# Four S5 output gates of layer 0 projected in the first stage, and the compressed queries cut into two jobs

## Chip, cores and metric

One Trainium2 chip, of which the kernel uses one core. The metric is the device time of one launch in microseconds (us), lower is better. Engines: PE (TensorE, matrix products and transposes), DVE (VectorE), ACT (ScalarE), POOL (GpSimd) and SP (SyncE), whose instruction stream issues nearly all DMAs. Every engine works through its own list in order; an instruction that waits holds up all that stand behind it on its engine.

## What is computed

A backbone of two layers over 512 latent tokens and 256 context tokens, width 1024, in float32. A layer feeds one modulated input to three branches: (A) a bidirectional S5 state-space layer with a GLU, (B) neighbourhood attention over an 8 x 64 grid with a learned bias, (C) latent attention (MLA) with compressed queries and keys. Each branch is projected to the model width, multiplied by a gate that is itself a projection of the input, and added:

```python
y = jax.nn.gelu(y)                                  # S5 output
y = y * jax.nn.sigmoid(y @ w_glu + b_glu)
...
IN_SPLITS = (SSM_WIDTH, SSM_WIDTH, NA_WIDTH, NA_WIDTH, NA_WIDTH, NA_WIDTH,
             MLA_Q_RANK, MLA_KV_RANK, MLA_ROPE_DIM, MLA_WIDTH, D_MODEL, D_MODEL, D_MODEL)
```

The last three slices of this projection are the gates of the branches. Then come an output projection, a residual and a layer norm. A second projection of the conditioning vector (`w_mod`) gives shift, scale and gate of each layer.

## The kernel before

**Numbers.** Each float32 operand is split into a high part (`hh`, `wh`, `ah`) and a low part (`hl`, `wl`, `al`), and a product is three matmuls (L232 for the projections, L1051 for the compressed ones). The high part is an ACT copy (L142), the low part a subtraction (L145) on DVE or POOL, as a table `SE` says for each stage; in the first stage of layer 0 every low part is DVE's. `wraw` (L215) loads 128 columns of weights into one of four `wr` buffers. A projection onto 128 channels is 8 x 3 matmuls of 512 columns and as many of 256.

**Stages of a layer.** First stage (`s5a`): projections of S5 inputs, gates and compressed queries, and, for layer 0, the S5 weight matrices, which DVE builds out of tables (tiles `sb`, with small PE products L659 and transposes L197 between them). Then neighbourhood attention and the S5 blocks (`na`), MLA (`mla`), the merge (`mrg`) and the output stage (`out`, L1608). In layer 0 the first stage takes about the first 239 us, the merge some 280 us up to 990 us.

**First stage.** `JOBS` (L108) is a string of letters for each layer, worked through from left to right: `u` S5 inputs, `a` and `m` gates of channels that are stored to DRAM (`za`, `zm`), `B` one S5 build, `N` the tables of the attention bias, `c` half of the compressed queries. `compressed(half)` first projects (L1051) and copies to `ct`, then computes an RMS scale on DVE, transposes `ct` in four groups on PE and stores the results (`rms_c` to `c`, `kpe` to `kr`).

**Merge of layer 0.** Branch b, then branch c, in eight steps each. Of the eight S5 gates (`ga`, columns `C_GA`) two are projected in the MLA stage and six after the merge's branch c (L1514 to L1517, each stored to `ga_d`). `SIDE` (L85) is one letter per step: `B` a build for layer 1, `N` the bias tables of layer 1 (loads L361, stores L363 to `na_zd`), `G` the function `gelu` of the S5 output. `gelu` closes the pool that builds and bias tables use, and takes its tiles from that memory. For each of four blocks it loads `y` (L1470, two buffers), squares (ACT), scales (DVE, L154), multiplies (POOL, L145), takes tanh (ACT), makes `gf` in nine pieces (DVE, L148), and splits it into `ah` (ACT) and `al` (DVE). The GLU follows: four groups of 24 matmuls over those four blocks, each with tanh, a product with `za` and a split. Then branch a: eight groups of 24 matmuls, gated by `ga`. `mod_step()` puts one piece of layer 1's `w_mod` product on PE (L306, four matmuls per 512 KB load L304) after each gate or group.

**Order.** The kernel is written in the order of these jobs; a scheduler of the framework then orders each engine's list by its own estimate of when things are ready, so that neighbouring jobs are interleaved. The list is fixed before the launch.

Of the kernel before, what the change touches and what calls it, by code (L numbers as in the profile page):

```python
# [15 lines left out]
AF = mybir.ActivationFunctionType  # L16
# [9 lines left out]
TOK = LAT + CTX  # L26
# [3 lines left out]
C_GA, C_GN, C_GM = 4000, 5024, 6048  # L30
# [51 lines left out]
SE = {'out0': (2, (1,)), 'out1': (2, (1,)), 'mla0': (4, (0,)), 'mla1': (2, (1,)), 's5a1': (1, (0,)), 'mrg0': (1, (0,))}  # L82
SE_REST = (3, (0,))

SIDE = ('T....B.B..N...G.........', '................G.......')  # L85

GX = ((0, 0, 1, 1), (1, 1, 1, 0))

# [16 lines left out]
TO = ((1024,), (1024,), (512, 512), (512, 512))  # L105
CE = 'VVA'

JOBS = ('uuBaBmaBmBacmaNmc', 'maaBmmaBcamucuuu')  # L108


G_NA = "na_q0 na_kh0 na_kl0 s5_u s5_s0 s5_s1 s5_w s5_rc s5_o s5_mg s5_va s5_vb s5_vp na_vc na_v na_z na_a na_b na_p na_pt na_q1 na_kh1 na_kl1"
# [8 lines left out]
def build(tc, a, out):  # L120
    nc = tc.nc
    V, S, P, PE = nc.vector, nc.scalar, nc.gpsimd, nc.tensor
    Q, PQ = nc.sync, nc.gpsimd
# [7 lines left out]
    def T(p, shape, tag, bufs=1, dt=F32):  # L131
        if isinstance(p, dict):
            p = p.get(tag, p[None])
        return p.tile(list(shape), dt, name=tag, tag=tag, bufs=bufs)
# [6 lines left out]
    def act(o, i, f=AF.Copy, **kw):  # L141
        return S.activation(out=o, in_=i, func=f, **kw)  # L142
# [14 lines left out]
    dr = pool("dr", DRAM)  # L157
# [669 lines left out]
    with st:  # L827
# [10 lines left out]
        for l in range(DEPTH):  # L838
            need_ctx = l < DEPTH - 1
            n_tok = TOK if need_ctx else LAT  # L840
# [16 lines left out]
            def project(c, with_ctx):  # L857
                wh, wl = wsplit(wraw(wi[:, c:c + 128], 8))
                return gemm(wh, wl, h_parts(with_ctx))
# [14 lines left out]
            def mod_step():  # L874
                next(later, None)

            u_d = []
            where[0] = f"s5a{l}"
            with phase("s5a", 3, 2, 1, 1) as sa:
                reserve(sa, [128, TOK], "z", 2)  # L880
# [25 lines left out]
                if l == 0:  # L906
                    sc = mod_prep(sa)
                    with tc.tile_pool(name="pre", bufs=1, reuse_waits="tile") as pre:
# [72 lines left out]
                        for q in range(4):  # L981
                            PQ.dma_start(out=dcols[32 * q:32 * q + 16].rearrange("i l b x -> i (l b) x"),
                                        in_=a["ssm_d"].rearrange("l (y x q i) -> q i (l y) x", x=2, q=4, i=16)[q])
# [49 lines left out]
                def compressed(half):  # L1033
# [7 lines left out]
                    for kc in range(4):  # L1041
# [3 lines left out]
                        for kk in range(2):  # L1045
                            k = 2 * kc + kk
# [30 lines left out]
                    for b in range(2):  # L1077
                        P.tensor_copy(  # L1078
                            out=ct[:, :, NC + 16 * b:NC + 16 * b + 16].rearrange("p j (s e) -> p j s e", s=2),
                            in_=ct[:, :, 384 + 16 * b:400 + 16 * b].rearrange("p j (s e) -> p j s e", s=2)[:, :, ::-1])  # L1080
                    for i in (3, 2, 0, 1):
                        n = 128 * (sum(with_q) if i < 2 else 3)
                        m = 64 if i == 3 else 128
                        q = pss()
                        for j in range(n // 128):
                            transpose(q[0:m, 128 * j:128 * j + 128], ct[:, j, 128 * i:128 * i + m])
                        tok = slice(384 * half, 384 * half + n)
                        if i < 3:
                            r = T(sp, [128, 384], "rms_c", 2)[:, 0:n]
                            act(r, q[:, 0:n], scale=gq[:, i:i + 1])  # L1090
                            Q.dma_start(out=c_d[i][:, tok], in_=r)
                            continue
                        nl = min(LAT - 384 * half, 384)
                        pe_t = T(sp, [32, 384], "kpe_t")
                        s = slice(384 * half, 384 * half + nl)
                        kpe = T(sp, [32, 384], "kpe")
                        tt(V, kpe[:, 0:nl], q[0:32, 0:nl], rope[0:32, s], ALU.mult)
                        tt(V, pe_t[:, 0:nl], q[32:64, 0:nl], rope[32:64, s], ALU.mult)
                        tt(V, kpe[:, 0:nl], kpe[:, 0:nl], pe_t[:, 0:nl], ALU.add)
                        if nl < 384:  # L1100
                            act(kpe[:, nl:384], q[0:32, nl:384])
                        Q.dma_start(out=kr_d[:, tok], in_=kpe)

                jobs = {"u": input_s5, "a": gate_a, "m": gate_m, "c": compressed, "B": build_s5, "N": biases}
                done = dict.fromkeys(jobs, 0)
                if l == 0:
                    done["u"] = NU
# [9 lines left out]
            with phase("na", 2, 2, 2, groups=G_NA) as nap:  # L1117
                for t in ("q", "kh", "kl"):
                    reserve(nap, [128, 2, TOK], f"na_{t}0", 1, FR)
                for i in range(4):  # L1120
# [30 lines left out]
                    z = T(nap, [128, TOK], "na_z", 2)  # L1151
# [110 lines left out]

            where[0] = f"mla{l}"
            with phase("mla", 2, 2, 2, groups=G_MLA) as mp:
                ga = {}
                exps = {}

                def gate_s(m):
# [23 lines left out]
                f = early((128, TOK), c_d[2])  # L1292
# [17 lines left out]
                for k in range(2):  # L1310
                    f = early((128, n_tok), c_d[k][:, 0:n_tok])
# [3 lines left out]
                for t in range(6):  # L1315
                    o = psg()
# [4 lines left out]
                for i in range(4):  # L1321
                    z = T(mp, [128, TOK], "mla_z", 2)
# [15 lines left out]
                    for k in range(2):  # L1338
                        Q.dma_start(out=uqv[:, k, :, 0:96],
                                    in_=a["mla_w_uq"][l, 128 * k:128 * k + 128, 192 * i:192 * i + 192]  # L1340
                                    .rearrange("p (h n) -> p h n", h=2))
                    for b in range(2):
                        V.tensor_copy(
                            out=uq[:, :, 96 + 16 * b:112 + 16 * b].rearrange("p k (s e) -> p k s e", s=2),
                            in_=uq[:, :, 64 + 16 * b:80 + 16 * b].rearrange("p k (s e) -> p k s e", s=2)[:, :, ::-1])
# [74 lines left out]
            with phase("mrg", 4, 3, 0, 1, groups=G_MRG) as mg, contextlib.ExitStack() as es:  # L1420
# [100 lines left out]
                for m2 in range(2):  # L1521
                    wh, wl = wsplit(wraw(a["ssm_w_glu"][l, :, 256 * m2:256 * m2 + 256], 4))
                    for r in range(2):
                        m = 2 * m2 + r
# [7 lines left out]
                        z = T(gp, [128, TOK], "za", 2)[:, 0:n_tok]  # L1532
# [21 lines left out]
            with phase("outp", 4, 4, 0, groups=G_OUT) as op:  # L1554
# [11 lines left out]
                for v in range(2 if need_ctx else 1):  # L1566
                    t = T(op, [128, D], f"gate{v}")
                    Q.dma_start(out=t.rearrange("p (k n) -> p k n", k=8),
                                in_=bass.AP(tensor=gd.tensor, offset=gd.offset + v * 128, ap=[[0, 128], [256, 8], [1, 128]]))
# [20 lines left out]
                for tl in range(6 if need_ctx else 4):  # L1590
# [12 lines left out]
                    for n in cols:  # L1603
                        c = slice(c0, c0 + n)
                        o = psg()[:, 0:n]
# [11 lines left out]
                    if last and LE[tl] == "A":  # L1617
                        normalise_act(op, r, r, (mean, rstd))
                        for n in range(2):
                            c = slice(512 * n, 512 * n + 512)  # L1620
# [46 lines left out]
```

## Time and profile before

| | us |
|---|---|
| runs shown, median (lowest, highest) | 1797.0 (1796.72, 1801.12) |
| the profiled execution, its own time | 1799.89 |
| span of the profiled execution | 1798.1 |
| PE busy | 1661.2 (92%) |
| DVE busy | 1239.1 (69%) |
| ACT busy | 747.0 (42%) |
| POOL busy | 482.3 (27%) |

The profiled execution took 2.9 us more than the median of the runs. The span begins with the first instruction profiled; all times of places below count from there. The mean granted clock of PE was 0.972 of full speed; by slices it lies at 1.00 or near 0.50, which are its two levels, 2.4 and 1.2 GHz. A matmul's row holds the time until its result is out, so rows of PE overlap: a step from start to start is what one costs.

### The profile page before, as it was taken

Reading aid. Unit: us, or ns where it says so; the run is one execution under the profiler, and the core shown is the slowest. Engines: PE = TensorE matmul, PEld = TensorE weight load, DVE = VectorE, ACT = ScalarE, POOL = GpSimd, SP = SyncE. Lnnn points to the kernel's source line nnn. Section 1 sums busy time; section 2 is a strip of 40 time slices with the busy share of each in tenths; the row PEclk is TensorE's granted clock in tenths of the full one; section 3 lists DMA queues with packets and bytes.
Section 4 is the critical chain, followed back from the end, with each engine's and each line's share of the span. In section 5 each row is a group of like instructions: output and inputs, shape, how many; then the busy total and the mean of one; then the engine's idle time right before and its main releaser. Section 6 shows DMA issues by size and latency. Waiting matters only on the chain. (4 is left out here: it accounts for less than half of the span.)

```text
span 1798.1 us, 29033 instructions
## 1 busy us (share of the span) xinstructions
PE 1661.2 (92%) x10808; PEld 1390.0 (77%) x10808; DVE 1239.1 (69%) x2653; ACT 747.0 (42%) x1466; POOL 482.3 (27%) x353
## 2 busy tenths in 40 slices
PE   4899699999999999999799988999999999999996
PEld 2687588888878888877687766788888788778875
DVE  4999938767755564979367688828888665752257
ACT  4433243344365565222143345443334555643241
POOL 2000122323422101201313552013433211245382
PEclk9999799999999999999899999999999899999998
DMA  9557784344321222755747726664555322253462
GB/s 305 162 189 222 205 243 119 110 136 128 99 81 54 71 68 77 239 157 178 197 156 230 203 74 199 217 180 152 158 148 150 94 80 65 83 153 106 129 205 71
DMA packets 273076, 264.87 MB, mean 147 GB/s; under 512 B 70440, under 2 KB 227896, under 8 KB 272936
## 3 DMA queue, kind: packets, MB, share of 16 engines
q1 hardware_dynamic: 271736, 259.93, 48.8%
q0 software_dynamic: 1200, 3.10, 0.5%
q8 instruction: 85, 1.39, 0.3%
q14 instruction: 55, 0.45, 0.1%
HBM read 198.64 MB, written 68.53 MB: 149 GB/s over the span
## 5 line engine op out<-in xcount | busy, mean ns | idle before, releaser
L232 PE MATMUL g<-hh,wh 128*128 128x512 f32 (+1 forms) x1344 | 478.7, 357 | 19.8 <-ACT wh L142 12.3
L232 PE MATMUL g<-hl,wh 128*128 128x512 f32 (+1 forms) x1344 | 476.6, 355 | 3.0 <-POOL hl L145 1.5
L232 PE MATMUL g<-hh,wl 128*128 128x512 f32 (+1 forms) x1344 | 474.3, 354 | 0.9 <-DVE wl L145 0.9
L232 PEld LDWEIGHTS g<-hh,wh 128*128 128x128 f32 x1344 | 255.2, 190 | 60.3 <-ACT wh L142 13.2
L232 PEld LDWEIGHTS g<-hl,wh 128*128 128x128 f32 x1344 | 255.4, 190 | 39.1 <-DVE hl L148 2.6
L232 PEld LDWEIGHTS g<-hh,wl 128*128 128x128 f32 x1344 | 254.8, 190 | 36.0 <-DVE wl L145 2.1
L142 ACT ACTIVATE wh<-wr 128x1024 fp32r<-128x1024 f32 (+1 forms) x150 | 155.1, 1035 | 238.7 <-PE g L232 127.9
L145 POOL TENSOR_TENSOR wl<-wr,wh 128x1024 fp32r<-128x1024 f32 (+1 forms) x53 | 128.1, 2416 | 331.3 <-ACT wh L142 321.5
L145 DVE TENSOR_TENSOR wl<-wr,wh 128x1024 fp32r<-128x1024 f32 (+1 forms) x97 | 127.3, 1315 | 93.2 <-ACT wh L142 92.8
L232 PE MATMUL g<-al,wh 128*128 128x512 f32 (+1 forms) x336 | 120.2, 358 | 1.8 <-DVE al L145 1.8
L232 PE MATMUL g<-ah,wl 128*128 128x512 f32 (+1 forms) x336 | 118.6, 358 | 2.1 <-POOL wl L145 2.1
L232 PE MATMUL g<-ah,wh 128*128 128x512 f32 (+1 forms) x336 | 120.0, 362 | 0.0
L145 POOL TENSOR_TENSOR macc<-macc,g_t 128x768 f32<-128x768 f32 (+1 forms) x32 | 56.4, 1769 | 146.8 <-DVE g_t L148 146.8
L142 ACT ACTIVATE mla_pt<-s 128x384 f32<-128x384 f32 (+1 forms) x128 | 59.4, 475 | 86.8 <-PE s L197 86.2
L1377 DVE TENSOR_REDUCE mla_sm<-w 128x1 f32<-128x768 f32 (+1 forms) x80 | 67.9, 849 | 33.9 <-PE w L1375 32.8
L142 ACT ACTIVATE na_p<-w,na_sm 128x512 f32<-128x512 f32 (+1 forms) x80 | 50.9, 645 | 89.2 <-DVE na_sm L152 80.3
L232 PEld LDWEIGHTS g<-ah,wh 128*128 128x128 f32 x336 | 63.5, 190 | 14.4 <-issue 3.1
L232 PEld LDWEIGHTS g<-ah,wl 128*128 128x128 f32 x336 | 63.8, 190 | 12.6 <-POOL wl L145 3.3
L232 PEld LDWEIGHTS g<-al,wh 128*128 128x128 f32 x336 | 63.9, 190 | 12.3 <-DVE al L145 2.5
L142 ACT ACTIVATE mla_p<-w,mla_sm 128x768 f32<-128x768 f32 (+1 forms) x80 | 65.0, 813 | 4.7 <-DVE mla_sm L152 4.5
L1608 PE MATMUL g<-woh,hh 128*128 128x512 f32 (+1 forms) x168 | 64.1, 382 | 1.6 <-ACT woh L142 1.4
L1078 POOL COPY ct<-ct 128x48 f32<-128x48 f32 x8 | 5.3, 694 | 221.0 <-ACT rms_q L142 186.1
(351 smaller groups left out, 3550.1 us busy)
## 6 DMA issues: line engine op xcount, KB each, us to landing
wr<-in_w_in SPq DMA_DIRECT2D x104, 512.0 KB, 4.3
wr<-in_w_mod SPq DMA_DIRECT2D x32, 512.0 KB, 4.7
s_w<-s_w SPq DMA_DIRECT2D x32, 512.0 KB, 4.0
s_o<-s_o SPq DMA_DIRECT2D x16, 568.0 KB, 5.5
wr<-in_w_out SPq DMA_DIRECT2D x16, 512.0 KB, 3.6
s_o<-sb SPq DMA_DIRECT2D x12, 576.0 KB, 4.5
wr<-in_w_in SPq DMA_DIRECT2D x16, 416.0 KB, 4.8
s_rc<-s_r SPq DMA_DIRECT2D x16, 384.0 KB, 3.1
```

What stands on the lines that cost most here:

```text
L142: return S.activation(out=o, in_=i, func=f, **kw)
L145: return e.tensor_tensor(out=o, in0=x, in1=y, op=op)
L232: PE.matmul(o, w[:, k], x[:, k, 0:n], start=(k == 0 and i == 0), stop=(k == nk - 1 and i == 2))
L1078: P.tensor_copy(out=ct[:, :, NC + 16 * b:NC + 16 * b + 16].rearrange("p j (s e) -> p j s e", s=2), in_=ct[:, :, 384 + 16 * b:400 + 16 * b] ...
L1377: V.tensor_reduce(out=sm[:, 3:4], in_=q[:, k0:TOK], axis=AX.X, op=ALU.max)
L1608: PE.matmul(o, x[:, k, tok], w[k][:, c], start=(k == 0 and i == 0), stop=(k == 7 and i == 2))
```

## The change

Layer 0: two letters enter `JOBS`. `g` projects one S5 gate and stores it (four of them, channels 0 to 3), and `c` now stops after its projections; `k` does its scale, transposes and stores. Between a `c` and its `k` stands at least one projection. So the MLA stage projects channels 4 and 5, and the merge 6 and 7, two where there were six. `gelu` stands one letter earlier in `SIDE`. Layer 1: only the `c` and `k` are split. The number of matmuls is the same.

```diff
-SIDE = ('T....B.B..N...G.........', '................G.......')
+SIDE = ('T....B.B..N..G..........', '................G.......')
-JOBS = ('uuBaBmaBmBacmaNmc', 'maaBmmaBcamucuuu')
+JOBS = ('uuBaBmaBmBgacgkmgaNcgmk', 'maaBmmaBcakmucuuku')
...
+            ga = {}
             where[0] = f"s5a{l}"
...
+                    yield
                     for i in (3, 2, 0, 1):
...
+                started = []
+                def compress(half):
+                    started.append(compressed(half))
+                    next(started[-1])
+                def compress_end(half):
+                    next(started[half], None)
+                def gate_s5(b):
+                    z = T(sa, [128, TOK], "z", 2)
+                    for s, n, o in project(C_GA + 128 * b, need_ctx):
+                        act(z[:, s], o, AF.Tanh, scale=0.5)
+                    ga[b] = T(dr, [128, TOK], f"ga_d{l}{b}")
+                    Q.dma_start(out=ga[b][:, 0:n_tok], in_=z[:, 0:n_tok])
+                    mod_step()
-                jobs = {"u": input_s5, "a": gate_a, "m": gate_m, "c": compressed, "B": build_s5, "N": biases}
+                jobs = {"u": input_s5, "a": gate_a, "m": gate_m, "c": compress, "k": compress_end, "g": gate_s5,
+                        "B": build_s5, "N": biases}
...
-                ga = {}
```

How the lists move at three places. First DVE in the first stage of layer 0, from the sum (`sb`, 1152 columns) that the last build but one hands to PE, to the products of the last build. Before:

```order
L145 TENSOR_TENSOR sb<-sb 128x1152
L145 TENSOR_TENSOR sb<-s_ta_293,s_tb_295 128x384
L148 SCALAR_TENSOR_TENSOR rms_v<-rms_v 128x6
L145 TENSOR_TENSOR sb<-sb 128x1024
L145 TENSOR_TENSOR sb<-s_ta_293,s_tb_294 128x384
L145 TENSOR_TENSOR sb<-sb 128x384
L148 SCALAR_TENSOR_TENSOR rms_v<-rms_v 128x6
L145 TENSOR_TENSOR sb<-s_c_1745,s_p_247 128x1152
```

The same place in the change:

```order
L145 TENSOR_TENSOR wl<-wr,wh 128x832
L145 TENSOR_TENSOR sb<-sb 128x1152
L148 SCALAR_TENSOR_TENSOR z<-z,g 128x512
L145 TENSOR_TENSOR sb<-sb 128x1024
L145 TENSOR_TENSOR sb<-sb 128x384
L145 TENSOR_TENSOR wl<-wr,wh 128x832
L148 SCALAR_TENSOR_TENSOR z<-z,g 128x256
L145 TENSOR_TENSOR sb<-s_ta_293,s_tb_294 128x384
L145 TENSOR_TENSOR sb<-s_c_1745,s_p_247 128x1152
```

Two low parts of weights and the two halves of one gate's product (`z`) now stand between the last two builds. On PE, behind the last matmul of the second `c`, 96 matmuls of two projections (one `g`, one `m`) stand ahead of its twelve transposes of `ct`, and those ahead of the attention's first projection; before, the attention's first projection followed at once, with the transposes among its matmuls.

Second, SP in the merge, from the weights of the second gate that the merge keeps to the first loads of `gelu`. Before:

```order
L215 DMA wr<-in_w_in 128x8x128
L363 DMA na_zd_9052<-sb 48x480
L1517 DMA ga_d_9711<-g_t 128x768
L215 DMA wr<-in_w_in 128x8x128 x2
L363 DMA na_zd_9052<-sb 48x480
L215 DMA wr<-in_w_in 128x8x128 x2
L1470 DMA y<-y_d_95 128x768
L1470 DMA y<-y_d_96 128x768
```

In the change:

```order
L215 DMA wr<-in_w_in 128x8x128
L363 DMA na_zd_9296<-sb 48x480
L1537 DMA ga_d_9955<-g_t 128x768
L215 DMA wr<-in_ssm_w_glu 128x4x256
L304 DMA wr<-in_w_mod 128x1024
L363 DMA na_zd_9296<-sb 48x480
L304 DMA wr<-in_w_mod 128x1024
L215 DMA wr<-in_ssm_w_glu 128x4x256
L1490 DMA y<-y_d_95 128x768
L1490 DMA y<-y_d_96 128x768
```

The loads of `y` (L1490 now) stand behind the same last two stores of bias tables and behind five weight loads of 512 KB as before; only which weights these are has changed.

Third, DVE at the end of `gelu`, blocks three and four. Before:

```order
L154 TENSOR_SCALAR y_t<-y_t 128x768
L148 SCALAR_TENSOR_TENSOR gf<-y_t,y 128x64 x8
L148 SCALAR_TENSOR_TENSOR gf<-y_t,y 128x8x32
L148 SCALAR_TENSOR_TENSOR gf<-y_t,y 128x64 x8
L148 SCALAR_TENSOR_TENSOR gf<-y_t,y 128x8x32
L145 TENSOR_TENSOR al_9496<-gf,ah_9495 128x768 x2
L145 TENSOR_TENSOR wl<-wr,wh 128x1024 x3
L148 SCALAR_TENSOR_TENSOR gf<-g_t,gf 128x768
```

In the change:

```order
L148 SCALAR_TENSOR_TENSOR gf<-y_t,y 128x64 x8
L148 SCALAR_TENSOR_TENSOR gf<-y_t,y 128x8x32
L154 TENSOR_SCALAR y_t<-y_t 128x768
L145 TENSOR_TENSOR al_9646<-gf,ah_9645 128x768
L148 SCALAR_TENSOR_TENSOR gf<-y_t,y 128x64 x8
L148 SCALAR_TENSOR_TENSOR gf<-y_t,y 128x8x32
L145 TENSOR_TENSOR mod_72<-s,mod_b 128x2x4 x2
L335 COPY mod_g<-s 16x128
L145 TENSOR_TENSOR al_9646<-gf,ah_9645 128x768
L148 SCALAR_TENSOR_TENSOR gf<-g_t,gf 128x768
```

The fourth block's low part now stands behind the end of the `w_mod` product, which waits for PE. Before, three weight splits stood between the last `al` and the GLU's first product; now none does. On PE, before, 240 matmuls of five gates stood between the wait for the second gate's weights and the GLU; now 48 of one gate do, then 16 matmuls of `w_mod`, then the GLU's first two groups over blocks one to three, with 16 more of `w_mod` among them, then the rows of `w_mod`'s end, then block four.

## Rows read from the trace of the kernel before

**Rows 1.** The page, busy time of each engine over the span.
```profile
PE 1661.2 (92%) x10808; PEld 1390.0 (77%) x10808; DVE 1239.1 (69%) x2653; ACT 747.0 (42%) x1466; POOL 482.3 (27%) x353
```

**Rows 2.** Busy time by stretches: PE, PEld, DVE, ACT, POOL, then clock, DMA, GB/s.
```profile
180.00:200.00 20.00, 14.15 (x105) 12.14 (x104) 19.64 (x37) 6.75 (x12) 0.00 (x0) 0.90 0.68 224
200.00:220.00 20.00, 9.08 (x61) 7.46 (x62) 18.65 (x26) 5.80 (x12) 4.19 (x2) 0.50 0.83 210
```

**Rows 3.** PE in order of time, last builds, second compressed job, start of attention.
```profile
203.98 1.08 PE L659 MATMUL s<-sb,s_b 128*32 128x128 f32 x16 [9.36 <-DVE sb L145]
213.95 1.08 PE L659 MATMUL s<-sb,s_b 128*32 128x128 f32 x16 [6.25 <-DVE rms_v L148]
218.68 0.72 PE L1051 MATMUL w<-wh,hh 128*128 128x416 f32 x1
...
229.73 0.46 PE L1051 MATMUL w<-wh,hh 128*128 128x416 f32 x1 [3.01 <-ACT wh L142]
...
238.64 0.39 PE L232 MATMUL g<-hh,wh 128*128 128x512 f32 x1
```

**Rows 4.** PE in order of time, one projection: its first matmul and the next projection's.
```profile
164.67 0.49 PE L232 MATMUL g<-hh,wh 128*128 128x512 f32 x1
...
173.12 0.40 PE L232 MATMUL g<-hh,wh 128*128 128x512 f32 x1
```

**Rows 5.** DVE in order of time, first stage: a low part, a gate's product, the last sum.
```profile
176.04 1.21 DVE L145 TENSOR_TENSOR wl<-wr,wh 128x1024 fp32r<-128x1024 f32 x1
...
190.70 0.67 DVE L148 SCALAR_TENSOR_TENSOR z<-z,g 128x512 f32<-128x512 f32 x1
...
212.45 1.35 DVE L145 TENSOR_TENSOR sb<-sb 128x1152 f32<-128x1152 f32 x1
```

**Rows 6.** PE in order of time, merge: second gate, GLU, 48 matmuls of branch a, output stage.
```profile
887.54 0.79 PE L232 MATMUL g<-hh,wh 128*128 128x512 f32 x1 [9.21 <-ACT wh L142]
...
932.32 0.50 PE L232 MATMUL g<-ah,wh 128*128 128x512 f32 x1
...
963.24 0.50 PE L232 MATMUL g<-ah,wh 128*128 128x512 f32 x1
...
971.72 0.27 PE L197 MATMUL s<-ident,mod_row 128*128 128x128 f32 x1
...
990.16 0.40 PE L1608 MATMUL g<-woh,hh 128*128 128x512 f32 x1
```

**Rows 7.** SP's queue in order of time, last bias store and the loads of y.
```profile
885.31 2.02 SPq L363 DMA_DIRECT2D na_zd<-sb  x1
...
889.18 2.33 SPq L1470 DMA_DIRECT2D y<-y_d  x2
```

**Rows 8.** The line L1470 by itself, its four loads of 384 KB.
```profile
DMA to landing us min/median/max: 2.9/4.2/5.5
```

**Rows 9.** ACT, POOL and DVE in order of time, gelu's operations.
```profile
896.42 1.57 ACT L142 ACTIVATE y_t<-y 128x768 f32<-128x768 f32 x2
...
899.81 0.85 ACT L142 ACTIVATE y_t<-y_t 128x768 f32<-128x768 f32 x1
...
900.28 2.75 POOL L145 TENSOR_TENSOR y_t<-y_t,y 128x768 f32<-128x768 f32 x1 [0.50 <-DVE y_t L154]
909.63 1.85 POOL L145 TENSOR_TENSOR y_t<-y_t,y 128x768 f32<-128x768 f32 x1 [6.60 <-DVE y_t L154]
...
901.25 5.84 DVE L148 SCALAR_TENSOR_TENSOR gf<-y_t,y 128x64 f32<-128x64 f32 x18
906.92 2.05 DVE L145 TENSOR_TENSOR al<-gf,ah 128x768 fp32r<-128x768 f32 x2
909.00 0.56 DVE L154 TENSOR_SCALAR y_t<-y_t 128x768 f32<-128x768 f32 x1
...
918.60 2.06 DVE L145 TENSOR_TENSOR al<-gf,ah 128x768 fp32r<-128x768 f32 x2
```

**Rows 10.** Busy time by stretches, columns as in rows 2, behind PE's 9.21 us wait.
```profile
890.00:895.00 5.00, 5.00 (x19) 3.94 (x18) 1.22 (x1) 0.30 (x1) 0.00 (x0) 0.75 1.16 324
```

## Prediction, made before the changed kernel was run

> **What bounds the kernel now.** The page comes first: PE is busy 92% of the span and no other engine over 69% [rows 1], so PE work that is moved is worth something only where PE waits, and the question is where it is taken from and where it is put. The stretches of the first stage come next [rows 2]: from 180 to 220 us DVE is busy 19.64 and 18.65 us of 20, while PE falls to 14.15 and 9.08 us, at a clock of 0.90 and then 0.50. There DVE's builds set the pace. PE in order of time shows the holes: 9.36 and 6.25 us, both ended by DVE, and 3.01 us ended by an ACT copy [rows 3]. The second compressed job starts when the last build has gone through (218.68) and ends at 238.64, where attention begins. In the merge PE has one hole, 9.21 us before its second gate, and then runs without a wait worth naming from 887.54 through five gates to the GLU at 932.32 and the output stage at 990.16 [rows 6]. Under those five gates lies all of gelu: loads of `y` from 889.18 [rows 7], squares, products, pieces and splits, the last of them over at 920.66, more than 11 us before the GLU [rows 9]. So the change takes PE work out of a stretch where it hides a chain, and puts it into one that has holes but whose end DVE sets.
>
> **What one gate costs.** One projection takes PE 8.45 us from its first wide matmul to the next one's (164.67 to 173.12) [rows 4], or 0.176 us a matmul. Four gates are 33.8 us. Each also costs DVE one low part of 1.21 us [rows 5], one ACT copy, one load and one store.
>
> **First stage, +18 us (15 to 21.5).** Three of the four gates stand ahead of the second compressed job, and one gate projection `m` has moved behind it, so 16.9 us more work than before stands there. The holes of 9.36 and 6.25 us and smaller ones before them [rows 3] hold most of it, and the rest pushes PE later only where DVE is later still. On the PE list 58 of these matmuls stand directly in the old 9.36 us hole: at 0.176 us they take about 10 us, and the hole closes. Nothing is put into the 6.25 us hole, so PE goes on waiting there, at the lower clock. What matters is when DVE is ready with the last build, at 212.45 before [rows 5]. Against that stand two more low parts (2 x 1.21) and, since `mod_g`, an end piece of `w_mod`, now waits on DVE for a PE transpose behind 24 gate matmuls, some 1.1 us of waiting; the product `z` of the moved `m` (0.67 us for its wider half, about 1.1 for both) has gone behind it. Sum +2.4: the last build is ready near 215, and the compressed job starts near 221.1. Its own 19.96 us hold a wait of 3.01 us [rows 3] for a copy queued behind a store's landing; it may stay or go, and I take half, -1.5. Its end then lies near 239.5, about where it was. Behind it the list has a gate and `m`, two whole projections that nothing covers: +16.9. Then come the twelve transposes, which used to stand among the attention's matmuls; their number is the same, and I take 0 for the wait that they now have to themselves (bounds -0.5 and +2). Sum: 2.4 - 1.5 + 16.9 = +17.8, say **+18**. If the wait stays and the transposes wait it is 21.5; if the wait goes and DVE loses less, 15. So of 33.8 us put in, about 16 are absorbed.
>
> **Attention and MLA of layer 0, 0 (-2 to +1.5).** Same work in the same order; the S5 loads at its head are issued behind the last stores of the compressed part, as late relative to it as before.
>
> **Merge, -17 us (-21 to -11).** Up to the second kept gate nothing moves: its weights stand behind the bias loads as before, so the hole of 9.21 us stays and the gate ends near 896. Title and table say that gelu is moved up. On SP it isn't: its first loads stand behind the same bias store, issued at 885.31, and the same number of weight loads (order, second place), because gelu's tiles take the memory of the bias tables. So `y` is loaded at 889.18 as before [rows 7], and with a landing of up to 5.5 us [rows 8] from the second issue near 891 it is there near 896.4, when ACT squared it before [rows 9]. What the four gates covered is now bare. The chain, by durations of rows 9: two squares to 898; scale, product and tanh of block one, and nine pieces of `gf`, half of 5.84, to about 903.6; one weight split (1.22) that now stands before block two's pieces; both `gf` by 907.7, both `al` (2.05) by 909.7. The other two loads of `y` need the buffers of the first two; issued near 904 and 908, they land before they are asked for. Block three: scale 0.56, product 1.85, tanh 0.85, pieces 2.92: 916. Block four, whose scale stands behind those pieces: 0.5 + 2.0 + 0.85 + 2.92 = 922.2. Then DVE's list has the `w_mod` end ahead of the last `al` (order, third place); its PE rows wait for nothing but block three, so about 1 us, and `al` is done near 924.3. PE has done in its waits the `w_mod` matmuls and block one to three of the GLU's first two groups. Eight matmuls of block four follow (1.4 us, 2.8 at the lower clock), then half of the GLU, 48 matmuls, 8.48 us (963.24 to 971.72 [rows 6]), a wait of about 2 us for the fourth group's products and split, and 192 matmuls of branch a, 4 x 8.48 = 33.9. That ends near 972. PE was mostly idle from 896, and after the 9.21 us hole, with PE busy again since 887.54, the clock was still 0.75 over the stretch from 890 to 895 [rows 10]; that is a loss of 1.25 us there, and as PE has some work from 917 on, I add 1 us. 973 against 990.16: **-17**.
>
> The one price that a page gives otherwise is that of the loads. The Trainium skill, "DMA: Bandwidth & Descriptors", section "Anatomy of one DMA", puts a DMA at 2.0 us plus its bytes over 436 GB/s (fitted for the GpSimd path; these go by SP), as an estimate 2.9 us for 384 KB. The fastest of the four loads agrees (2.9), the slowest, in the crowd that matters here, took 5.5 [rows 8]. By the page's price gelu would start 2.6 us sooner and the whole sum would be 2.6 us lower.
>
> **Layer 1, 0 (-1.5 to +1.5).** Compressed job and end are split there too, with projections between that only change places, and none of layer 1's gates or of its gelu moves.
>
> **Sum.** 18 + 0 - 17 + 0 = +1 us. Against the profiled execution's 1799.9 us that is 1800.9; the median of the runs lies 2.9 us lower, so 1798. A measurement of this kernel tells about 0.3% (5.4 us) from no change, and that is what I forecast: **no change**, with 1798 us. Its own range, all terms together: -8 to +13 at the extremes, which will not come together; 1790 to 1806.
>
> **Rivals.** *Faster: the gaps fill better.* The compressed job no longer waits, the builds lose nothing to the added splits because DVE had 1.35 us of every 20 free at the end [rows 2], and `y` lands after 2.9 us. Then the first stage costs 15 and the merge gives 20: -5 to -9, about 1790. For it: the lists leave PE 58 matmuls ready for the hole. Against: DVE's rows there are back to back, and the loads of `y` go out amid a DMA share of 1.16 [rows 10].
>
> *Slower: gelu's last loads come late.* In the change the merge's end hangs on gelu, and each microsecond of it is one of the kernel; before, it had 11 us to spare [rows 6, 9]. The loads of `y` for blocks three and four now stand on SP behind loads of `w_mod` and of branch a, each of which waits until PE or DVE has emptied a `wr` buffer, and PE in turn waits for `w_mod` loads to land. Place: the fourth block's load. I have it issued near 908. If two such waits come one after the other, each with a landing like those of rows 8 (4.2 us), it is issued near 916 and lands near 920; then square, scale, product, tanh and pieces follow bare (0.85 + 0.56 + 1.85 + 0.85 + 2.92 = 7.0), and the last `al` is ready near 929.5. For it: the list has four such loads ahead of the third block's and two more ahead of the fourth's, where it had one ahead of both. Against: the buffers should be free by 905. It decides from an issue at 915 on; the kernel is then at 1804 to 1808.
>
> *The change doesn't do what it says.* For gelu's letter that is already in the sum: at the same place in SP's queue it is worth nothing. If the loads did start with the letter, one step of branch c earlier (a gate and 24 matmuls, 8.45 + 4.24 = 12.7 us), the merge would end near 961 and the kernel at 1786; the list speaks against it.
>
> **How the numbers follow.** No change 0.40, as the two large terms cancel to within the bounds of either. Faster by over 0.3%: 0.31 (gaps 0.28, gelu early 0.03). Slower: 0.29 (the late load 0.18; the first stage at its upper bound with the merge at -15, 0.11). The range that holds 8 in 10 reaches into both sides: 1785 to 1811.
>
> **What would show it.** In the changed profile: attention's first projection 15 to 21 us later than 238.64; in the first stage the 9.36 us wait gone and a wait of 6 to 8 us before the last L659 still there; in the merge a gate, then waits that sum to some 17 us within 30 us, ended by DVE's `gf` and `al`; the output stage's start at most 4 us from 990. Wrong it would be if the last build's sum comes before 213 or after 218, if `y` is loaded well before the gate starts, or if the GLU's second half starts before 922 or after 932.

## The result, and the profile after

The change made the kernel slower: 1822.24 us (median; 1814.13 to 1829.81) against 1798.28 us (1796.72 to 1801.12) for the kernel before, a ratio of 1.0131 with an interval of 1.0083 to 1.0178. The forecast was 1798, with 1785 to 1811 as its range. The profiled execution took 1829.81 us, with a span of 1828.0; it is the slowest of the four, so the stages below add up to more than the medians differ by.

The page's busy times answer to [rows 1]. PE is busy 18 us longer for the same 10808 matmuls, and the span is 30 us longer:

```profile
PE 1679.4 (92%) x10808; PEld 1405.3 (77%) x10808; DVE 1234.8 (68%) x2651; ACT 748.2 (41%) x1466; POOL 492.0 (27%) x355
```

Where the 30 us lie is read from four stretches of each kernel. First those of the kernel before: last builds up to the attention's first projection; attention up to the MLA's first product; the first load of `y` up to the output stage; and layer 1 from the scan's first product to its MLA's first. Columns: the stretch, its length, then busy PE, PEld, DVE, ACT and POOL, then the clock, the DMA share and GB/s:

```profile
150.00:238.64 88.64, 65.73 (x405) 57.54 (x403) 71.73 (x110) 29.69 (x58) 13.15 (x10) 0.83 0.76 221
238.64:521.30 282.66, 269.76 (x2050) 233.98 (x2049) 202.61 (x406) 122.94 (x276) 89.61 (x80) 0.99 0.47 134
889.18:990.16 100.98, 99.81 (x593) 83.75 (x592) 65.16 (x96) 40.49 (x60) 24.42 (x11) 0.98 0.65 205
1213.50:1441.30 227.80, 218.83 (x1622) 189.82 (x1623) 184.49 (x328) 93.66 (x187) 81.67 (x73) 0.97 0.48 140
```

The same stretches of the changed kernel:

```profile
150.00:261.07 111.07, 95.94 (x603) 84.46 (x602) 81.42 (x137) 43.81 (x91) 20.39 (x11) 0.94 0.73 210
261.07:550.80 289.73, 271.84 (x2036) 237.56 (x2036) 205.78 (x387) 116.35 (x255) 90.47 (x78) 0.97 0.45 129
919.00:1004.86 85.86, 75.42 (x400) 59.80 (x399) 56.65 (x94) 33.40 (x49) 24.69 (x12) 0.84 0.60 198
1224.44:1470.30 245.86, 230.56 (x1633) 198.77 (x1634) 186.76 (x324) 94.24 (x187) 80.86 (x74) 0.92 0.45 129
```

The first stage is 22.4 us longer, the attention of layer 0 is 7.1 longer, the merge 15.1 shorter, and layer 1's attention, in which the change edits nothing, some 18 longer. Length less PE busy is PE's idle time: 22.9, 12.9, 1.2 and 9.0 us before, 15.1, 17.9, 10.4 and 15.3 after. So of the 33.8 us put into the first stage 11.4 were absorbed, not 16: its waits fell by 7.8 us, and its clock rose from 0.83 to 0.94. Two attentions gained waits.

PE in order of time, where [rows 3] stood before. The last field of a row is the idle time ahead of it and what ended it:

```profile
209.07 0.65 PE L659 MATMUL s<-sb,s_b 128*32 128x128 f32 x16 [0.44 <-DVE sb L145]
...
220.40 1.08 PE L659 MATMUL s<-sb,s_b 128*32 128x128 f32 x16 [8.44 <-DVE sb L145]
...
225.13 0.72 PE L1052 MATMUL w<-wh,hh 128*128 128x416 f32 x1
...
241.35 0.39 PE L232 MATMUL g<-hh,wh 128*128 128x512 f32 x1
...
259.95 0.87 PE L197 MATMUL s<-ident,ct 128*128 128x128 f32 x6 [1.11 <-ACT rms_c L142]
...
261.07 0.50 PE L232 MATMUL g<-hh,wh 128*128 128x512 f32 x1 [0.25 <-DVE z L148]
```

The 9.36 us wait is closed. The one before the last build's products has grown from 6.25 to 8.44 us, and behind the compressed job (225.13 to 241.35) stand 16.7 us of a gate and `m`, then 3.05 us of transposes (258.02 to 261.07).

In the merge, PE in order of time, from the `w_mod` matmuls behind the gate to the output stage [rows 6]; at 952.76 begins block four of the GLU's first two groups, at 956.92 the GLU's second half:

```profile
932.81 1.08 PE L306 MATMUL m<-wr,mod_sc 128*32 128x256 f32 x8 [2.47 <-DMA wr<-in_w_mod]
...
936.77 0.79 PE L232 MATMUL g<-al,wh 128*128 128x512 f32 x1 [1.30 <-DVE al L145]
...
944.74 0.64 PE L306 MATMUL m<-wr,mod_sc 128*32 128x256 f32 x8 [1.57 <-DMA wr<-in_w_mod]
...
947.25 0.80 PE L232 MATMUL g<-al,wh 128*128 128x512 f32 x1 [0.98 <-DVE al L145]
...
952.73 0.38 PE L197 MATMUL s<-ident,mod 128*16 128x128 f32 x1 [0.34 <-DVE mod L145]
952.76 1.63 PE L232 MATMUL g<-ah,wh 128*128 128x512 f32 x4
954.34 0.79 PE L232 MATMUL g<-al,wh 128*128 128x512 f32 x1
...
956.92 0.40 PE L232 MATMUL g<-ah,wh 128*128 128x512 f32 x1
...
973.83 1.65 PE L232 MATMUL g<-ah,wh 128*128 128x512 f32 x4 [2.11 <-ACT ah L142]
...
1004.86 0.40 PE L1628 MATMUL g<-woh,hh 128*128 128x512 f32 x1
```

### The profile page after: what moved, and what is told of

Its sections match the earlier page's. It is cut to its first block, busy times and chain, and to the rows that moved or that the text cites. A ratio compares the mean times of both kernels' runs of the same rounds, so it can differ in the third digit from the quotient of the medians.

```text
span 1828.0 us, 29040 instructions
## 1 busy us (share of the span) xinstructions
PE 1679.4 (92%) x10808; PEld 1405.3 (77%) x10808; DVE 1234.8 (68%) x2651; ACT 748.2 (41%) x1466; POOL 492.0 (27%) x355
## 5 line engine op out<-in xcount | busy, mean ns | idle before, releaser
L232 PE MATMUL g<-hh,wh 128*128 128x512 f32 (+1 forms) x1344 | 482.6, 360 | 23.4 <-ACT wh L142 11.7
L232 PEld LDWEIGHTS g<-hh,wh 128*128 128x128 f32 x1344 | 258.3, 192 | 65.3 <-ACT wh L142 12.5
L142 ACT ACTIVATE wh<-wr 128x1024 fp32r<-128x1024 f32 (+2 forms) x150 | 155.1, 1036 | 259.9 <-PE g L232 162.4
L232 PEld LDWEIGHTS g<-ah,wl 128*128 128x128 f32 x336 | 66.1, 197 | 13.5 <-DVE wl L145 2.4
L232 PEld LDWEIGHTS g<-ah,wh 128*128 128x128 f32 x336 | 64.7, 196 | 15.1 <-ACT ah L142 3.5
L1079 POOL COPY ct<-ct 128x48 f32<-128x48 f32 x8 | 13.2, 1685 | 225.4 <-DVE ct L1067 157.1
```

The source lines that it names most:

```text
L232: PE.matmul(o, w[:, k], x[:, k, 0:n], start=(k == 0 and i == 0), stop=(k == nk - 1 and i == 2))
L1079: P.tensor_copy(out=ct[:, :, NC + 16 * b:NC + 16 * b + 16].rearrange("p j (s e) -> p j s e", s=2), in_=ct[:, :, 384 + 16 * b:400 + 16 * b] ...
```

## The experiments

"MLA 0" is the first product of layer 0's MLA, against 521.3 us in the profile before; "merge" the time from the first load of `y` to the output stage, against 100.98; "layer 1" from its scan to its MLA, against 227.8. These three come from one profile each, set against the one profile before; the ratio comes from all the runs, set against those of the kernel before on the same chip.

| run | MLA 0 | merge | layer 1 | ratio (95% interval) |
|---|---|---|---|---|
| the change | +29.5 | -15.1 | +18.0 | 1.0131 (1.0083 to 1.0178) |
| e1_again | +27.2 | -18.6 | +6.7 | 1.0094 (1.0067 to 1.0120) |
| e2_phase_kept | +28.2 | -17.1 | +2.6 | 1.0076 (1.0055 to 1.0096) |
| e3_before_phase | -1.1 | +0.4 | +7.7 | 1.0078 (1.0054 to 1.0103) |
| e4_l1_cut | +0.2 | 0.0 | +1.4 | 1.0000 (0.9980 to 1.0019) |
| e5_l0_cut | +9.7 | -0.9 | +2.0 | 1.0058 (1.0040 to 1.0076) |
| e6_gates_uncut | +28.1 | -17.6 | -0.2 | 1.0053 (1.0036 to 1.0070) |
| e7_two_gates | +18.9 | -15.5 | +1.0 | 1.0060 (1.0037 to 1.0083) |
| e8_no_mod_in_gate | +27.3 | -19.0 | +0.3 | 1.0063 (1.0041 to 1.0085) |
| e9_four_early | +8.2 | -15.4 | +2.8 | 0.9958 (0.9941 to 0.9974) |
| e10_four_pool | +11.9 | -17.5 | +1.5 | 0.9964 (0.9943 to 0.9984) |
| e11_two_pool | +4.8 | -15.6 | +2.6 | 1.0012 (0.9998 to 1.0027) |
| e12_four_early_drift | +8.7 | -17.9 | +4.6 | 0.9941 (0.9922 to 0.9961) |

One profile of a stage is not exact to a microsecond. e3 and e4 have layer 0 as in the kernel before, instruction for instruction on PE, DVE, ACT and POOL. e3's first two stretches:

```profile
150.00:234.71 84.71, 62.35 (x401) 54.49 (x400) 68.80 (x110) 28.90 (x57) 13.21 (x10) 0.86 0.75 223
234.71:520.22 285.51, 273.13 (x2049) 237.40 (x2048) 202.57 (x406) 122.96 (x276) 89.62 (x80) 0.98 0.46 134
```

In e4 they are 86.43 and 285.08 us long. Against these two the first stage of the profile before is 2 to 4 us longer and its attention 2.4 to 2.9 us shorter, while the MLA's start agrees within 1.1 us.

**Layer 1: what reaches it.** `split` decides by a counter that runs through the whole program which engine makes a low part; outside the stages named in `SE` every third goes to DVE, the others to POOL:

```python
flip[0] += 1
n, dve = SE0 if where[0] == "s5a0" else SE.get(where[0], SE_REST)
e = V if flip[0] % n in dve else P
```

It is set to 1 ahead of layer 0's attention and then never again. The merge that loses four gates counts four splits fewer, so layer 1's attention deals its low parts otherwise, and the scheduler gives that stage another order on every engine. Four runs on one chip: the change as it is; the change with the four counts put back (e2); the kernel before with the counter moved to the same remainder (e3); the kernel before with layer 1's `c` and `k` cut and nothing else (e4). In runs where a job is not cut, its `k` follows its `c` at once.

```diff
             if l == 0:
                 flip[0] = 1
+            else:
+                flip[0] += 4
```

That is e2; e3 is the kernel before with `+= 2` in that place, and e4:

```diff
-JOBS = (..., 'maaBmmaBcamucuuu')
+JOBS = (..., 'maaBmmaBcakmucuuku')
```

> The changed kernel once more, unaltered. Its four times so far spread over 1814 to 1830 us, the profiled one being the slowest, with the first stage +22 us, layer 0's attention +7, the merge -17 and layer 1's attention +18 against the kernel before. Theory A (something lasting in layer 1's attention costs time): that stage is again 10 us or more above the 241 us of before, total near 1820. Rival B (the spread is a matter of the single execution): layer 1's attention is near 241 in this profile and the total near 1812.

> The changed kernel, but the counter that deals low parts out in turn to DVE and POOL is advanced by 4 ahead of layer 1's attention, as the four gates that left the merge would have done. Theory A1 (the counter's lost steps change which low parts of layer 1's attention go to DVE and which to POOL, and that costs the 18 us): layer 1's attention back to 241 us within 3, total 1802 to 1808. Rival A2 (what was moved in layer 0, or the compressed job's cut in layer 1, costs them): no gain, total near 1820.

> The kernel before, with only that counter advanced by 2 ahead of layer 1's attention, which gives the dealing that the change has there; no gate moves and no job is cut. Theory A1: layer 1's attention +10 to +18 us, total 1808 to 1816. Rival A2: no change, 1797 to 1800.

> The kernel before, with only layer 1's compressed job cut in two (its job string as changed). Theory A1: within 3 us of the kernel before, since the dealing stays. Rival A2 in its layer 1 form (the cut costs it): 8 us or more slower.

Layer 1's cut costs nothing (1.0000). The kernel before with the shifted counter is 0.78% slower, with nothing else edited, and by the order of instructions its layer 1 attention is that of the change on PE and DVE. PE in order of time in layer 1's attention, first e3, the kernel before with the counter shifted:

```profile
1294.92 0.44 PE L760 MATMUL w<-s_s,s_o 128*128 128x64 f32 x2 [2.15 <-DVE s_s L145]
...
1331.12 0.43 PE L759 MATMUL w<-s_s,s_o 128*128 128x64 f32 x2 [2.28 <-DVE s_s L145]
...
1398.83 0.43 PE L759 MATMUL w<-s_s,s_o 128*128 128x64 f32 x2 [3.34 <-DVE s_s L145]
```

and the change:

```profile
1308.04 0.48 PE L760 MATMUL w<-s_s,s_o 128*128 128x64 f32 x2 [2.15 <-DVE s_s L145]
...
1349.74 0.69 PE L759 MATMUL w<-s_s,s_o 128*128 128x64 f32 x2 [2.29 <-DVE s_s L145]
...
1418.78 0.69 PE L759 MATMUL w<-s_s,s_o 128*128 128x64 f32 x2 [3.34 <-DVE s_s L145]
```

Both show the same three waits for the scan's `s_s`; the longest three of the kernel before there are 1.06, 1.37 and 1.24 us. No single wait marks the order, though: e1, the change again, has the last two (2.28 and 3.34 us) but 0.42 in place of the first, and e2, e5, e8 and e9, whose order is that of the kernel before but for a few rows, each have one wait for `s_s` of 3.09 to 3.76 us. What tells the orders apart is the sum. In e3 the stage has 16.1 us of PE idle time (235.5 long, 219.4 busy), in the change 15.3, in e1 12.8, in the kernel before 9.0, and in e2 and e4 to e11 6.0 to 11.2. The other 11.7 of the change's 18 us are busy time, at a clock of 0.92 over the stretch against 0.97 before. Putting the counts back (e2) brings the stage to +2.6 us, within what that order, but for a few rows, gives in runs e4 to e11 (-0.2 to +2.8). In the ratio e1 and e2 overlap, so e2's gain shows in the profiles and not in the times; what is left, some 13 us, lies in layer 0. Some forecasts missed: e1 came between its two theories (+6.7 us, 1814 us in all), e3's stage took less than the +10 forecast, and e2's total of 1810 us lies above its 1808.

**Layer 0: the cut, the gates, or the number of gates.** All four runs have layer 1 as in the kernel before (uncut, the counter put back).

The letters of layer 0 (for e5 the first line is that of the kernel before, and gelu keeps its place; for e6 and e7 that of the change); then e8, in `gate_s5`:

```diff
-uuBaBmaBmBacmaNmc
+uuBaBmaBmBacmkaNcmk
...
-uuBaBmaBmBgacgkmgaNcgmk
+uuBaBmaBmBgackgmgaNckgm
...
-uuBaBmaBmBgacgkmgaNcgmk
+uuBaBmaBmBgacgkmaNcmk
...
-                    mod_step()
```

> The kernel before with nothing but layer 0's compressed queries cut in two jobs (c, a projection, k): no gate moves, gelu stays, layer 1 is untouched and its counter keeps its phase. Theory A (the gates' own work is what the first stage pays for, the cut is nearly free): layer 0's attention starts within 2 us of before, the run ends within 3 us of before. Theory B (the cut, with c's second part behind a projection, is what makes the first stage longer): the attention starts 6 to 10 us later and the run ends 6 to 10 us later. Theory C (the attention of layer 0 is slower because the scheduler gives it other lists once its entry changes): its lists change here as well, so from the s5 scan's first product to the MLA's first it takes 5 to 8 us more, and the run ends so much later, although the first stage is as long as before.

> All four gates moved and gelu a letter earlier, but no compressed query is cut in either layer, and the counter of the low parts is set on by 4 ahead of layer 1's attention, so that layer 1 has the lists of before. Theory A: first stage +20 to +24, merge -15 to -18, end +6 to +12, as in the run with the phase kept. Theory B (the cut is at fault): first stage +10 to +14, end -4 to +2. Theory C: besides A's numbers +5 to +8 between the s5 scan and the MLA of layer 0.

> Only two of the four gates moved (one ahead of the last build's products, one between the second c's halves cut by it), layer 0 cut, layer 1 uncut, counter set on by 2. Theory A with the merge bound by VectorE (the changed kernel's tail of the merge stands still for 15 us behind gf and al, into which two gates of 8.45 us would fit): first stage +9 to +13, merge still -14 to -17, so the end is -6 to +2 with the attention of layer 0 unchanged and up to +8 with C's extra. Rival (the merge gives back per gate moved): first stage +9 to +13, merge -7 to -9, end +2 to +10.

> The changed kernel with layer 1 uncut and the counter set on by 4, and without the step of the modulation's products that each moved gate takes along in the first stage (they are taken later). Theory A' (the last build's sum slips from 215 to 219 us because VectorE takes the modulation's additions first, behind the gate's 24 products): the last build's transposes start 3 to 5 us earlier than in the changed kernel, the attention 3 to 5 us earlier, and the end is 3 to 5 us under the run with the phase kept, unless the steps cost as much in the merge. Rival (the slip comes from the gates' products ahead of the build's own on TensorE): attention within 1.5 us of the changed kernel, end within 2 us of the run with the phase kept.

Theory A, that the cut is nearly free and the gates alone cost, fell: with no gate moved, e5 loses 9.7 us up to the MLA. Theory B, that the cut does it, comes near in e5 itself (the attention starts 5.9 us later, the run ends 10.4 later by the ratio), but fell too: e6 cuts nothing and is as late at the MLA as the change. Theory C, that other lists slow the attention, is taken up with e9. What e5, e6, e7 and e8 have in common is neither: one or two projections stand behind the products of the second compressed job, where the kernel before has none. In e5 and e7 that is `m`, in e6 and e8 a gate and `m`. PE in order of time in e5:

```profile
202.09 1.08 PE L659 MATMUL s<-sb,s_b 128*32 128x128 f32 x16 [9.11 <-DVE sb L145]
...
210.88 1.08 PE L659 MATMUL s<-sb,s_b 128*32 128x128 f32 x16 [5.62 <-DVE sb L145]
...
232.10 0.40 PE L232 MATMUL g<-hh,wh 128*128 128x512 f32 x1
...
244.54 0.77 PE L232 MATMUL g<-hh,wh 128*128 128x512 f32 x1
```

The waits for DVE stay, and `m`, which used to stand ahead of them, now follows bare from 232.10. In e7 the merge gives back 15.5 us for two gates, all that it gives for four, as theory A said; but with one of its projections behind the compressed job it is no faster than the others, and its end, +10.7 us by the ratio, lies above both forecasts. In e8 the dropped call had no product left to issue in this place: its instructions are those of the change with layer 1 put back, in the same order. The run therefore tells nothing of the step of the modulation, and counts as one more of the change without layer 1's part: 1.0063.

**All gates ahead of the second compressed job.**

For e9 and e12 the letters of layer 0 are the first new line below. In both, and in e10, the first half is still cut, by a gate; the second stands whole at the end. e9 sets the counter on by 4, e12 doesn't. e10 is e9 with the low parts of the moved gates on POOL, and e11 is e10 with two gates (the second new line) and the counter set on by 2.

```diff
-uuBaBmaBmBgacgkmgaNcgmk
+uuBaBmaBmBgacgkgmgaNmck
...
+uuBaBmaBmBgackgmaNmck
...
-SE = {..., 'mrg0': (1, (0,))}
+SE = {..., 'mrg0': (1, (0,)), 's5g': (1, ())}
...
+                    where[0] = "s5g"
+                    parts = project(C_GA + 128 * b, need_ctx)
+                    where[0] = f"s5a{l}"
```

> All four gates moved, but every one of them ahead of the second compressed job, which ends the first stage whole, as it does in the kernel before (layer 0 'uuBaBmaBmBgacgkmgaNmck', layer 1 uncut, counter set on by 4, low parts on VectorE as in the change). By the order of instructions layer 0's attention then has the lists of before on every engine. Theory L (the attention of layer 0 loses its 4 to 7 us to the lists that the scheduler builds behind another tail of the first stage): the attention takes 282 to 284 us again up to the MLA's first product, and the end is +1 to +5 against before, 4 to 7 less than with the change's tail. Rival (the attention is slower for what the moved gates leave to it, transfers or the clock): it takes 287 to 290 as in the change and the end stays at +7 to +10.

> As the run with four early gates, but the low parts of the moved gates' weights are made on GpSimd and not on VectorE. Theory D (in the first stage VectorE is full from 150 to 214 us, so TensorE's waits there are VectorE's and no free room; each moved gate adds a low part of 1.21 us to it): the sum of the last build comes 3 to 6 us sooner than in the run with four early gates, the attention 3 to 6 us sooner, the end -3 to +1 against before. Rival P (the last build is late because the gates' 24 products stand ahead of its own on TensorE and ScalarE, low parts don't matter): attention and end within 1.5 us of the run with four early gates.

> Only two gates moved, both ahead of the second compressed job, nothing cut, their low parts on GpSimd, counter set on by 2; layer 0's attention has the lists of before but for a few rows. Theories D and L with the merge's standstill (15 us behind gf and al, which the two gates left there fill): first stage +2 to +8, attention 0 to +2, merge -14 to -17, end -13 to -6 against before, a ratio of .993 to .997. Rival (each gate pays in the first stage what it weighs, 5 to 6 us, as the four did): first stage +10 to +12, end -6 to -2. Rival (the lists are not it): as the run with two gates, end +3.

> The run with four early gates once more, but without the line that sets the counter of the low parts on by 4, so that layer 1's attention has the drifted order that the change gave it; up to there both kernels are the same. Theory F (the drift of the counter costs layer 1's attention time by itself): from the scan's first product of layer 1 to its MLA's first the kernel takes 6 to 18 us more than before where the run with four early gates takes 3 more, and the end is +4 to +15 above that run, a ratio to before of .998 to 1.004. Rival (the 18 us of the changed kernel's run were of that run, not of the drift): within 2 us of the run with four early gates, a ratio of .994 to .998.

e9 moves the same four gates and is 0.42% faster than the kernel before, where +1 to +5 us had been forecast. PE in order of time:

```profile
213.20 0.64 PE L659 MATMUL s<-sb,s_b 128*32 128x128 f32 x16
...
223.74 0.64 PE L659 MATMUL s<-sb,s_b 128*32 128x128 f32 x16
...
227.78 0.35 PE L1052 MATMUL w<-wh,hh 128*128 128x416 f32 x1
...
236.76 0.46 PE L1052 MATMUL w<-wh,hh 128*128 128x416 f32 x1 [1.30 <-ACT wh L142]
...
244.32 0.39 PE L232 MATMUL g<-hh,wh 128*128 128x512 f32 x1
```

and its first two stretches, as above:

```profile
150.00:244.32 94.32, 89.95 (x581) 79.69 (x581) 76.59 (x116) 36.92 (x69) 18.83 (x10) 1.00 0.77 236
244.32:529.50 285.18, 272.69 (x2050) 237.27 (x2049) 202.48 (x406) 123.06 (x276) 89.57 (x80) 0.98 0.47 135
```

Neither build's products wait any more. DVE begins the last build's sum at 217.35 us, hardly sooner than in the change (218.90), but PE arrives at 223.74 with work done instead of at 211.96 with none left. PE's idle time in the stretch falls from 22.9 us to 4.4, its clock rises from 0.83 to 1.00, and 33.8 us of projections lengthen it by 5.7 (by 8 to 10 against e3 and e4; up to the MLA it is 8.2, and 8.7 in e12). The merge gives its 15.4 us as in the change. The attention has the order of before on PE, DVE, ACT and POOL, and 12.5 us of idle time, as before (12.9), where the change has 17.9: theory L holds for those 5 us. Its length, 285.2 us, lies 2.5 over the profile before, but e3 and e4, with the same order, took 285.5 and 285.1.

e10 goes against theory D: without the gates' low parts on DVE the last build's sum begins 0.7 us later than in e9 (218.09), its products start only 1.3 us sooner (222.42), the attention 4.1 us later (248.38), and the ratio is that of e9 within the intervals. The rival had both times within 1.5 us, so for the attention it misses too. e11 misses its forecast. It is ahead by 8.9 us when the output stage starts and has lost 6.7 of these again by the end, in stages that its edits don't touch, 5.0 of them between the start of the output stage and layer 1's scan; why stays open. That two gates are too few for the first stage its trace does show: a wait of 7.12 us before the last build's products is still there.

```profile
219.70 1.08 PE L659 MATMUL s<-sb,s_b 128*32 128x128 f32 x16 [7.12 <-DVE sb L145]
```

e12 went against theory F: 0.9941, no slower than e9, though its layer 1 attention took 4.6 us more than before in the profile, and e9's 2.8. Its layer 1 attention is neither that of the kernel before nor that of the change: from the same remainder of the counter the scheduler made a third order, and that one has none of the three waits shown. So the drift of the counter need not cost time by itself: it draws another order, and the change drew a worse one than e12. e9 and e12 beat both kernels, by 0.4 and 0.6% against the one before.

## Why the prediction was wrong

**"Layer 1, 0": wrong, the largest error.** "Projections between that only change places" is true of what is written there, and e4 confirms that the cut is free. But the counter and the scheduler carry layer 0's edit into layer 1: +18.0 us in the profiled execution, +6.7 and +7.7 in two more of that order. The order of the two kernels' instructions differs through all of layer 1's attention, which the instruction lists show; I had looked at the compressed jobs alone.

**"Attention and MLA of layer 0, 0 ... Same work in the same order": wrong.** It is the same work (2050 rows of PE before, 2036 after, twelve transposes having moved out), not the same order. The stage took 7.1 us more than in the profile before and 4.2 to 4.7 more than in e3 and e4; 5.0 us are waits of PE. The row below is the largest of them; the longest wait there in the kernel before is 2.16 us.

```profile
497.40 0.47 PE L197 MATMUL s<-ident,na_vc 128*128 128x128 f32 x1 [4.10 <-DVE na_v L1171]
```

**First stage, +18 (15 to 21.5): the mechanism was right, the size was not.** It was +22.4. The last build "ready near 215": its sum, which began at 212.45 before, began at 218.90, past the 218 that I had named as proof against it (216.8 to 219.3 in e1, e2, e6 and e8). DVE in order of time shows the larger part, two waits, 3.4 us in all, where I had put "some 1.1 us":

```profile
198.93 0.28 DVE L335 COPY mod_g<-s 16x128 f32<-16x128 f32 x1 [2.13 <-PE s L197]
...
200.51 2.63 DVE L145 TENSOR_TENSOR sb<-s_c,s_p 128x1152 f32<-128x1152 f32 x2 [1.30 <-ACT s_c L142]
```

The compressed job therefore started at 225.13 and not 221.1; it lost most of its own wait and took 16.2 us where I had 18.4. The bare gate and `m` took 16.7 for the 16.9 put down; the transposes, taken as 0 with +2 as bound, took 3.05. What I did not ask is whether those 16.9 us had to be bare. The text says "nothing is put into the 6.25 us hole" and treats it as given; e9 puts the two projections there and pays 5.7 us instead of 22.4 (8.2 instead of 29.5 up to the MLA).

**Merge, -17 (-21 to -11): right in size, in part by luck.** It was -15.1, and -15.4 to -19.0 in all other runs with gates moved. The gate started at 917.35 after a wait of 9.31 us and `y` was issued 1.65 us behind it, at 919.00, as before, so gelu's letter was worth nothing. From there to the last `al` the chain took 35.3 us where the sum had some 35, and the GLU's second half started after 37.9 (956.92) where it had 36.5 to 38. But two terms were off against each other. DVE in order of time, pieces of block four, end of `w_mod`, last `al`:

```profile
947.29 2.15 DVE L148 SCALAR_TENSOR_TENSOR gf<-y_t,y 128x64 f32<-128x64 f32 x9
952.43 0.25 DVE L145 TENSOR_TENSOR mod<-s,mod_b 128x8 f32<-128x8 f32 x2 [2.99 <-PE s L197]
...
953.36 0.93 DVE L145 TENSOR_TENSOR al<-gf,ah 128x768 fp32r<-128x768 f32 x1
```

Block four's `gf` was done 30.4 us behind the issue where I had 33, and the end of `w_mod` then held up the last `al` for 3.9 us where I had about 1. Nor did the "waits that sum to some 17 us" come. Between the gate and the GLU's second half they are 7.5 us, the two longest (2.47 and 1.57) ended by loads of `w_mod` and not by DVE. PE's work there ran at a low clock, for which I had added 1 us; the stretch, columns as above:

```profile
925.80:956.92 31.12, 23.65 (x138) 15.49 (x137) 19.45 (x49) 12.60 (x19) 7.32 (x4) 0.73 0.67 215
```

The four loads of `y` in the merge, line L1490 by itself as in [rows 8]:

```profile
DMA to landing us min/median/max: 5.1/5.8/6.4
```

My sum had taken up to 5.5 us. By the Trainium skill, page "DMA: Bandwidth & Descriptors", section "Anatomy of one DMA", an estimate for 384 KB, by a fit for the GpSimd path where these go by SP, is 2.9 us. None of these four loads came near it, and a sum lower by 2.6 us would have been further off.

**The rivals.** "Slower: gelu's last loads come late" would have given 1804 to 1808 by another mechanism, and it did not happen: the fourth block's load was issued at 936.01, 17.0 us behind the first, which on the clock of the profile before is 906.2 and not 915 or later. The outcome was slower through three terms at once, of which two had been given bounds of no more than 2 us. "-8 to +13 at the extremes" (the bounds add up to -9.5 and +13.5) could not hold it.

## What to carry to other kernels

A hole that another engine ends takes in only work that stands ahead of the waiting instruction in its engine's list. Four projections placed there cost some 6 to 10 us of 33.8, by the profile that they are set against; two of them left behind the last wait are paid in full. And where a scheduler orders the lists, a stage that nobody edited is not a stage that stays the same: compare its order as well, look for counters and entry conditions that run through the program, and give such a stage bounds from what a different order has cost elsewhere.

## What the runs showed of the chip that I had not expected

The same list with the same waits does not always get the same clock. e3 has the order of the change in layer 1's attention and the three waits shown above, within 0.01 us. In the change PE's mean clock over that stretch was 0.92 of full speed and PE was busy for 230.56 us; in e3:

```profile
1212.11:1447.60 235.49, 219.42 (x1632) 188.55 (x1633) 184.29 (x323) 93.58 (x186) 82.53 (x74) 0.98 0.46 135
```

That is 11.1 us less for the same matmuls. It may have to do with the spread of the times, 1814 to 1830 us in the change's first four runs and 1800 to 1820 in the ten of e3, against 1792 to 1802 in the ten of e4; but the kernel before, too, spread from 1789 to 1803 in 29 runs, and no run here shows the link.
